# Two of a sample's four loads issued by ScalarE, the small constants sent behind the first weights, and a later place for one block's inverse root

## The chip, the cores and the metric

The kernel runs on one core of a Trainium2 chip. The metric is the device time of one execution in microseconds (us). A core has five engines with a queue of instructions each: TensorE (PE in the profile; its weight loads are PEld), VectorE (DVE), ScalarE (ACT), GpSimd (POOL) and SyncE (SP). SP here only issues DMA transfers; ScalarE and GpSimd can issue them too. An engine runs its queue in order: an instruction that waits holds up all behind it.

## The reference

One encoder layer is applied to a prompt of 1,024 tokens and to a sample of 256 tokens, with one set of weights, all in float32:

```python
h = rmsnorm(x, norm_mix_w)                 # x * rsqrt(mean(x*x) + 1e-6) * w
proj = h @ w_in                            # DeltaNet q/k/v, gates, sg_u, sg_v, branch gates
y_a = deltanet_branch(...) @ w_up_a
y_b = spatial_gating_branch(sg_u, sg_v, ...) @ w_up_b
x = x + (sigmoid(gate_a) * y_a + sigmoid(gate_b) * y_b) @ w_out
x = x + memory_cross_attention(rmsnorm(x), rmsnorm(mem), ...)
x = x + swiglu(rmsnorm(x))                 # then a final rmsnorm
```

Only the very beginning matters here: the first `rmsnorm` of the tokens, the projections to `sg_v` and `sg_u`, and the layer norm and token mixing of the spatial gating branch.

## The kernel before

**Tiling.** Activations lie with features on the 128 partitions: a block of tokens is eight tiles of 128 features by up to 512 tokens. There are three blocks: 0 and 1 are the prompt's halves (512 tokens each), block 2 is the sample (256 tokens). Float32 products are made from three products of a rounded part (`hi`) and a remainder (`lo`) of each operand. `split` (L124) makes them: `hi` on ScalarE, `lo` on VectorE or GpSimd, so every normalised tile takes a VectorE product (L288, tile `nt`), a ScalarE rounding (L125, `hi`) and a subtraction (L126, `lo`).

**The order of the work.** TensorE runs in the order in which the program is written. The other engines' orders are made by a planner, which works from the written order and its own idea of when an operand is ready and may let a ready instruction pass one that it thinks is not. Within the part called `begin` (L399 to L448) ScalarE, GpSimd and VectorE keep the written order among their own instructions there, though the planner can put others between them. The main stream of matmuls is a generator. After each group of matmuls it hands over to `pump` (L71), which runs the side jobs that are due. Due times go by a written clock, `K.clock`, that counts TensorE's time only: a matmul of 264 columns adds 264/2.4 = 110 units, one of 512 columns 213. A side job that yields 2800 goes on after matmuls worth 2,800 units have been written.

**The beginning (L374 to L448).** SP loads the sample `xs` in four transfers of two feature tiles each (L376, 256 KB each), then `sm` (L389, 54.5 KB: norm weights and other small constants), then the first half of the `sg_v` weights in two transfers (`sv_raw0`, L361, 528 KB each), the second half (`second`), block 0 (`x0`, L355) and other constants (`cst`, L394). ScalarE squares the four parts of `xs` (L404), TensorE sums them into means (L413), and ScalarE and VectorE make the inverse root (L416, then three steps L419 to L421). In between, ScalarE splits the first `sg_v` weights (L417, seen as L125 with tile `svh`). Then each of the sample's eight tiles is multiplied by a column of `sm` and the root (L431), rounded (L432) and subtracted (L436), and TensorE starts on real products as they arrive. Before that TensorE is given products of zeros (`hold`, L384). A later line, L479, halves nine columns of `sm` on VectorE. It is written after `begin`, and nothing of the beginning needs its result. Transfers take turns on eight completion semaphores, so each waits for the one that was eight before it.

**The norms of the prompt's blocks.** `other_norms` (L452) is one side job that normalises block 0, block 1 and the memory tokens one after the other. For block 1 and the memory it calls `norm` (L306): eight tiles are squared and added up (`nacc`), and then `rest` (L256) writes small matmuls that sum over partitions (L267), VectorE's root (L270, then ten short steps L225 to L229, result `nst`), a pause `lag2`, matmuls that spread the root over all partitions (L275, shown as `bank<-cst,nst`), and the eight tiles' products and splits, one every 900 units for block 1. `rest` has 2800 as the default of `lag2`; `norm` doesn't set it.

**The main stream beside it.** `sgv(b)` (L571) multiplies a block by the `sg_v` weights, in two halves, one chunk of 128 tokens after the other; each chunk is eight groups of three matmuls and then a GELU (L484 to L487). It is followed by `sgu(0, b)` and `sgu(1, b)` (24 matmuls of 512 columns each). Blocks come in the order 2, 0, 1. `sgv(1)` reads block 1's `hi` and `lo`; `until` (L95) lets side jobs run on until block 1 is marked done. After `sgv(b)` the side job `ln` (L503) normalises that block's chunks: short VectorE steps, a squaring per chunk on ScalarE (L511, `junk`), a root, and a product per chunk on VectorE (L516, `vg`). `mix` (L618) then multiplies `vg` by the token mixing matrix (L625, `bank<-sw,vg`), written 8,000 units after block 0's `ln` is done.

Of the kernel before, what the change touches and what calls it, by code (L numbers as in the profile page):

```python
# [20 lines left out]
NP, NS = 1024, 256  # L21
# [16 lines left out]
S_MIX, S_XA, S_MEM, S_FFN, S_FIN, S_CONV, S_DNW, S_LNW, S_LNB = 0, 8, 16, 24, 32, 40, 100, 101, 105  # L38
# [16 lines left out]
class Trunk:  # L55
# [68 lines left out]
    def split(self, hi, lo, src, eng=None):  # L124
        self.last_hi = self.nc.scalar.activation(hi, src, AF.Copy).ins  # L125
        (eng or self.nc.vector).tensor_tensor(out=lo, in0=src, in1=f32(hi), op=ALU.subtract)  # L126
# [37 lines left out]
def trunk_kernel(ctx: ExitStack, tc: tile.TileContext, a):  # L164
    nc = tc.nc
    V, S, G, T, SY = nc.vector, nc.scalar, nc.gpsimd, nc.tensor, nc.sync
# [3 lines left out]
    def pool(name, bufs=1, **kw):  # L170
        if kw.get("space") != DRAM:
            kw["reuse_waits"] = "tile"
        return tc.tile_pool(name=name, bufs=bufs, **kw)
# [12 lines left out]
    n = 0  # L186
# [31 lines left out]
    def bank(p=pq, tag="b"):  # L218
        return p.tile([P, 512], F32, tag=tag, name="bank")
# [83 lines left out]
        rsqrt(y, ms, sc)  # L303
        yield lag2

    def norm(p, xk, n, wcol, sink, pace=1300, step=700, lag=1500):  # L306
        nm = Norm(p, n)
        for k in range(KT):
            nm.add(xk(k))
            yield step  # L310
        yield from nm.rest(xk, wcol, sink, pace, lag=lag)

    def to_h(h, b):
        return lambda k, t: split(h[b][0][:, k, :], h[b][1][:, k, :], t, V if k % 2 else G)

    def act_tiles(p=None):

        p = p or hp
        return [
            (  # L320
                p.tile([P, KT, n], F32R, tag=f"hi{b}", name=f"hi{b}"),
                p.tile([P, KT, n], F32R, tag=f"lo{b}", name=f"lo{b}"),
            )
            for b, (_, n) in enumerate(BLOCKS)
        ]
# [23 lines left out]
    xp = ses.enter_context(pool("xin"))  # L349
    sv = []  # L350

    def x_load(src, t0, n, name):
        x = xp.tile([P, KT, 512], F32, tag="x", name=name)[:, :, :n]
        for k in range(0, KT, 2):
            SY.dma_start(x[:, k : k + 2, :], src[:, k : k + 2, t0 : t0 + n])  # L355
        return x

    def sv_raw(half, raws=None):
        raws = [K.raw() for _ in range(2)] if raws is None else raws
        for i, raw in enumerate(raws):  # L360
            SY.dma_start(raw, a["w_sv"][half][:, i * 1056 : (i + 1) * 1056])  # L361
        return raws
# [10 lines left out]

    xs = hp.tile([P, KT, NS], F32, tag="lo1", name="xs")  # L374
    for k in range(0, KT, 2):
        SY.dma_start(xs[:, k : k + 2, :], a["xT"][:, k : k + 2, NP:])  # L376
    h05 = cp.tile([P, 13], F32, name="h05")
    fixed = h05[:, 9:12]
    for i, v in enumerate((1.0 / D, EPS, 0.0)):
# [4 lines left out]
    def hold(n, room):  # L384
        for _ in range(n):
            T.matmul(room, zero.to_broadcast([P, P]), zero.to_broadcast([P, room.shape[1]]), start=True, stop=True)

    hold(3, bank())
    SY.dma_start(sm, a["small"])  # L389
    sv_raw0 = sv_raw(0)  # L390
    second = hp.tile([P, 2, 1056], F32, tag="hi1", name="second")
    sv_raw1 = sv_raw(1, [second[:, i, :] for i in range(2)])
    x0 = x_load(a["xT"], 0, 512, "x0")
# [2 lines left out]
    x_h = act_tiles()  # L396
# [28 lines left out]
    for k in range(KT):  # L425
# [8 lines left out]
        while los and (k == KT - 1 or los[0][0] < k):  # L434
            n, t = los.pop(0)
# [16 lines left out]
    def other_norms():  # L452
        nm = Norm(xp, 512)
        nm.acc = squares[:, 0, :]
        yield from nm.rest(lambda k: x0[:, k, :], S_MIX, to_h(x_h, 0), 600, lag=LAG0, halves=2)
        done.add(0)
        x1_ = x_load(a["xT"], 512, 512, "x1")
        yield 3000
        yield from norm(xp, lambda k: x1_[:, k, :], 512, S_MIX, to_h(x_h, 1), 900, lag=4500)
        done.add(1)  # L460
        mem = x_load(a["memT"], 0, 512, "mem")
        yield 6000
        yield from norm(xp, lambda k: mem[:, k, :], 512, S_MEM, lambda k, t: SY.dma_start(md[k], t))

    norms = K.side(other_norms())


# [1990 lines left out]
```

## Time and profile before

| | us |
|---|---|
| median of 3 runs | 2195.53 (2195.31 to 2195.96) |
| the profiled execution | 2195.64 |
| its span, first to last instruction | 2193.9 |
| PE busy in the span | 2176.9 (99%) |
| DVE, ACT, POOL busy | 1357.6, 880.1, 572.9 |
| granted TensorE clock (share of full speed) | 0.999 |

The profiled execution's time is 1.74 us more than its span, what lies around the first and last instruction. "Busy" of PE counts from the start of a matmul to its modelled end, and consecutive matmuls overlap, so the real rate is read from the distance between starts. In a timeline row the columns are start, length, engine, line, operation, written and read tiles with their shape, the number of instructions that were merged, and in brackets the engine's idle time before it with what ended it. Transfers issued by an engine appear as that engine with a "q" (SPq, ACTq); their length is that of issuing, not of moving the data.

### The profile page before, as it was taken

Reading aid. Unit: us, or ns where it says so; the run is one execution under the profiler, and the core shown is the slowest. Engines: PE = TensorE matmul, PEld = TensorE weight load, DVE = VectorE, ACT = ScalarE, POOL = GpSimd, SP = SyncE. Lnnn points to the kernel's source line nnn. Section 1 sums busy time; section 2 is a strip of 40 time slices with the busy share of each in tenths; the row PEclk is TensorE's granted clock in tenths of the full one; section 3 lists DMA queues with packets and bytes.
Section 4 is the critical chain, followed back from the end, with each engine's and each line's share of the span. In section 5 each row is a group of like instructions: output and inputs, shape, how many; then the busy total and the mean of one; then the engine's idle time right before and its main releaser. Section 6 shows DMA issues by size and latency. Waiting matters only on the chain.

```text
span 2193.9 us, 32384 instructions
## 1 busy us (share of the span) xinstructions
PE 2176.9 (99%) x12436; PEld 1905.0 (87%) x12436; DVE 1357.6 (62%) x2614; ACT 880.1 (40%) x1648; POOL 572.9 (26%) x379
## 2 busy tenths in 40 slices
PE   9999999999999999999999999999999999999998
PEld 8888888898888899888988888888888888888888
DVE  7868587686874845677644546644434444378575
ACT  6433262544535453124544433332322222343454
POOL 3010010100000000042412332566666665200031
PEclk9999999999999999999999999999999999999999
DMA  5221412323234546741522421222222222493631
GB/s 194 92 93 57 118 54 94 82 66 93 75 119 124 169 138 209 238 144 43 188 68 107 162 98 63 102 84 87 82 77 77 85 96 91 138 347 125 206 111 58
DMA packets 188309, 255.13 MB, mean 116 GB/s; under 512 B 71978, under 2 KB 102266, under 8 KB 188154
## 3 DMA queue, kind: packets, MB, share of 16 engines
q1 hardware_dynamic: 170618, 228.15, 31.7%
q10 hardware_dynamic: 17536, 24.91, 3.1%
q8 instruction: 97, 1.59, 0.3%
q14 instruction: 58, 0.48, 0.1%
HBM read 179.05 MB, written 73.97 MB: 115 GB/s over the span
## 4 chain that ended last, share of the span: by engine, by line
PE 90%; DVE 4%; ACT 2%; DMA 1%; issue 1%; POOL 0%; DVEq 0%; SPq 0%; ACTq 0%
PE bank L108 89%; PE bank L121 1%; DVE acc L689 1%; DVE U L931 1%; DMA braw<-gq 1%; DVE zt L923 0%; ACT U L913 0%; ACT UT L910 0%; ACT hi L125 0%; DVE lo L126 0%; DVE gb L810 0%; DVE gs L689 0%; ACT acc L687 0%; ACT gs L692 0%; ACT whi L125 0%
## 5 line engine op out<-in xcount | busy, mean ns | idle before, releaser
L108 PE MATMUL bank<-hi,whi 128*128 128x512 f32 (+1 forms) x1976 | 701.7, 355 | 0.2 <-DVE vg L487 0.2
L108 PE MATMUL bank<-hi,wlo 128*128 128x512 f32 (+1 forms) x1976 | 687.1, 348 | 0.0
L108 PE MATMUL bank<-lo,whi 128*128 128x512 f32 (+1 forms) x1976 | 686.9, 348 | 0.0
L108 PEld LDWEIGHTS bank<-hi,wlo 128*128 128x128 f32 x1976 | 373.5, 189 | 48.7
L108 PEld LDWEIGHTS bank<-hi,whi 128*128 128x128 f32 x1976 | 374.4, 189 | 44.8 <-DVE vg L487 1.0
L108 PEld LDWEIGHTS bank<-lo,whi 128*128 128x128 f32 x1976 | 374.6, 190 | 43.1
L125 ACT ACTIVATE whi<-raw 128x1024 fp32r<-128x1024 f32 (+1 forms) x136 | 136.9, 1009 | 252.5 <-PE bank L108 225.1
L126 POOL TENSOR_TENSOR wlo<-raw,whi 128x1024 fp32r<-128x1024 f32 x65 | 159.5, 2455 | 290.4 <-ACT whi L125 290.4
L108 PE MATMUL bank<-bhl,whi 128*128 128x512 f32 x408 | 125.9, 390 | 0.0
L126 DVE TENSOR_TENSOR wlo<-raw,whi 128x1024 fp32r<-128x1024 f32 (+1 forms) x71 | 80.7, 1139 | 69.5 <-ACT whi L125 66.8
L126 POOL TENSOR_TENSOR wlo<-x,whi 128x1024 fp32r<-128x1024 f32 x40 | 97.5, 2436 | 46.7 <-ACT whi L125 46.7
L2091 DVE TENSOR_TENSOR x<-x,bank 128x512 f32<-128x512 f32 x21 | 14.4, 688 | 124.3 <-ACT x L1886 124.3
L689 DVE SCALAR_TENSOR_TENSOR acc<-craw,sm,acc 128x510 f32<-128x510 f32 (+1 forms) x96 | 73.8, 769 | 27.6 <-ACT acc L687 25.9
L108 PEld LDWEIGHTS bank<-bhl,whi 128*128 128x128 f32 x408 | 76.4, 188 | 16.4 <-ACT whi L125 0.4
L1899 DVE SCALAR_TENSOR_TENSOR t<-t,x 128x512 f32<-128x512 f32 x42 | 64.4, 1534 | 28.4 <-ACT t L1898 28.4
L125 ACT ACTIVATE whi<-x 128x1024 fp32r<-128x1024 f32 (+1 forms) x48 | 49.2, 1026 | 78.1 <-PE bank L108 70.1
L108 PE MATMUL bank<-bhl,wlo 128*128 128x512 f32 x204 | 79.6, 390 | 0.5 <-DVE wlo L126 0.5
L1908 DVE SCALAR_TENSOR_TENSOR t<-bank,t 128x512 f32<-128x512 f32 (+1 forms) x44 | 24.5, 558 | 82.6 <-PE bank L108 82.6
L108 PE MATMUL bank<-bhl,ahl 128*128 128x512 f32 x312 | 75.0, 395 | 0.0
L1050 ACT ACTIVATE gs<-bank 128x512 f32<-128x512 f32 (+1 forms) x60 | 31.2, 519 | 102.9 <-PE bank L108 93.5
L108 PEld LDWEIGHTS bank<-bhl,ahl 128*128 128x128 f32 x312 | 58.7, 188 | 13.6
L1886 ACT ACTIVATE x<-bank 128x512 f32<-128x512 f32 x63 | 37.6, 597 | 82.0 <-PE bank L108 79.8
(411 smaller groups left out, 4517.3 us busy)
## 6 DMA issues: line engine op xcount, KB each, us to landing
raw<-in_w_gu SPq DMA_DIRECT2D x44, 512.0 KB, 3.3
braw<-gq SPq DMA_DIRECT2D x14, 1024.0 KB, 7.5
raw<-in_w_g SPq DMA_DIRECT2D x20, 512.0 KB, 3.3
gq<-t SPq DMA_DIRECT2D x33, 256.0 KB, 2.1
gtd<-gs ACTq DMA_DIRECT2D x32, 256.0 KB, 2.3
w<-in_w_dn SPq DMA_DIRECT2D x8, 1024.0 KB, 12.6
raw<-in_w_qkv SPq DMA_DIRECT2D x12, 512.0 KB, 3.4
gq<-r SPq DMA_DIRECT2D x22, 256.0 KB, 2.0
```

The lines of the kernel that those rows point to most:

```text
L108: self.nc.tensor.matmul(out, l, r, start=start, stop=stop, skip_group_check=more)
L121: self.nc.tensor.transpose(out, x, ident)
L125: self.last_hi = self.nc.scalar.activation(hi, src, AF.Copy).ins
L126: (eng or self.nc.vector).tensor_tensor(out=lo, in0=src, in1=f32(hi), op=ALU.subtract)
L689: V.scalar_tensor_tensor(out=dst, in0=src, scalar=wj, in1=dst, op0=ALU.mult, op1=ALU.add)
L931: V.scalar_tensor_tensor(out=U[d][:, hs, :], in0=quad(pu), scalar=mine[:, 2 * level + d : 2 * level + d + 1], in1=U[d][:, hs, :], op0=ALU. ...
L1050: S.activation(t, ps, AF.Tanh, scale=0.5)
L1886: S.activation(t, ps, AF.Copy)
L1899: V.scalar_tensor_tensor(out=t, in0=t, scalar=1.0, in1=src, op0=ALU.add, op1=ALU.mult)
L1908: V.scalar_tensor_tensor(out=out, in0=u, scalar=sign, in1=t, op0=ALU.mult, op1=ALU.mult)
L2091: V.tensor_tensor(out=c22, in0=c22, in1=pe, op=ALU.add)
```

## The change

The second and fourth load of `xs` are issued by ScalarE in place of SP. The load of `sm` moves behind the two loads of `sv_raw0` in SP's order. `norm` takes the pause `lag2` as an argument, 2800 by default, and block 1's call sets it to 5000, so that the spreading matmuls and all that follows them in that side job are written later. Block 0 (which calls `rest` directly) and the memory tokens keep 2800.

```diff
-    def norm(p, xk, n, wcol, sink, pace=1300, step=700, lag=1500):
+    def norm(p, xk, n, wcol, sink, pace=1300, step=700, lag=1500, lag2=2800):
         nm = Norm(p, n)
         for k in range(KT):
             nm.add(xk(k))
             yield step
-        yield from nm.rest(xk, wcol, sink, pace, lag=lag)
+        yield from nm.rest(xk, wcol, sink, pace, lag=lag, lag2=lag2)
...
     for k in range(0, KT, 2):
-        SY.dma_start(xs[:, k : k + 2, :], a["xT"][:, k : k + 2, NP:])
+        (S if k % 4 else SY).dma_start(xs[:, k : k + 2, :], a["xT"][:, k : k + 2, NP:])
...
     hold(3, bank())
+    sv_raw0 = sv_raw(0)
     SY.dma_start(sm, a["small"])
-    sv_raw0 = sv_raw(0)
     second = hp.tile([P, 2, 1056], F32, tag="hi1", name="second")
...
-        yield from norm(xp, lambda k: x1_[:, k, :], 512, S_MIX, to_h(x_h, 1), 900, lag=4500)
+        yield from norm(xp, lambda k: x1_[:, k, :], 512, S_MIX, to_h(x_h, 1), 900, lag=4500, lag2=5000)
```

## The prediction

> **What bounds the kernel now.** The page first, for how much there is to win:
>
> ```profile
> span 2193.9 us, 32384 instructions
> PE 2176.9 (99%) x12436; PEld 1905.0 (87%) x12436; DVE 1357.6 (62%) x2614; ACT 880.1 (40%) x1648; POOL 572.9 (26%) x379
> ```
>
> TensorE sets the time. All its idle time is 2193.9 - 2176.9 = 17.0 us, 0.8% of the span, so a change that only moves work can win no more than that, and this one touches the first 100 us. The waits of PE in the first 130 us come next (total, times, longest):
>
> ```profile
> PE bank L108 <- DVE ab L607: 1.6, 1, 1.6
> ...
> PE bank L108 <- POOL lo L126: 0.7, 1, 0.7
> ...
> PE bank L108 <- DVE vg L516: 0.4, 1, 0.4
> ```
>
> Which wait is whose is read from the timeline. The beginning, up to the first real product:
>
> ```profile
> 0.73 1.28 ACT L382 ACT_TABLE_LOAD   x1 [0.73 <-PEq L2446]
> 0.74 1.97 SPq L376 DMA_DIRECT2D xs<-in_xT  x4
> 2.75 0.47 SPq L389 DMA_DIRECT2D sm<-in_small  x1
> 3.26 0.91 SPq L361 DMA_DIRECT2D raw<-in_w_sv  x2
> 3.52 1.39 ACT L404 ACTIVATE first<-xs 128x512 f32<-128x512 f32 x2 [1.29 <-DMA xs<-in_xT]
> 6.30 1.37 ACT L404 ACTIVATE first<-xs 128x512 f32<-128x512 f32 x2 [1.39 <-DMA xs<-in_xT]
> 7.32 0.17 DVE L479 TENSOR_SCALAR h<-sm 128x9 f32<-128x9 f32 x1 [1.69 <-DMA sm<-in_small]
> 9.07 0.47 ACT L416 ACTIVATE seed<-bank,h 128x256 f32<-128x256 f32 x1 [1.41 <-PE bank L108]
> 9.26 0.76 SPq L394 DMA_DIRECT2D cst<-in_const  x1
> 9.45 2.21 ACT L125 ACTIVATE svh<-raw 128x1056 fp32r<-128x1056 f32 x2
> 9.58 0.43 DVE L419 SCALAR_TENSOR_TENSOR bank<-bank,seed 128x256 f32<-128x256 f32 x1 [2.09 <-ACT seed L416]
> 10.98 0.88 DVE L431 SCALAR_TENSOR_TENSOR bank<-xs,sm,bank 128x256 f32<-128x256 f32 x2
> 11.56 0.72 ACT L432 ACTIVATE hi<-bank 128x256 fp32r<-128x256 f32 x2
> 11.98 0.51 PE L108 MATMUL bank<-svh,hi 128*128 128x264 f32 x2 [0.42 <-ACT hi L432]
> ```
>
> Two chains meet at 11.56. One is the sample's: third quarter of `xs` at 6.30, squares, means, root (9.07), three VectorE steps, first product with `sm` (10.98). The other is ScalarE's splitting of the first weights, 9.45 to 11.66. `sm` itself landed by 7.32, and L479, which nobody here needs, took it while VectorE had nothing to do.
>
> How fast the loads come, as the issue list of the first 30 us (size, median us to landing) and the busy shares of two stretches (last column GB/s) have it, and what issuing costs ScalarE later in the kernel (ns, least/median/most):
>
> ```profile
> raw<-in_w_sv SPq DMA_DIRECT2D x2, 528.0 KB, 6.4
> ```
> ```profile
> 1.75:2.50 0.75, 0.75 (x2) 0.34 (x1) 0.00 (x0) 0.47 (x2) 0.00 (x0) 1.00 0.67 139
> 2.50:3.75 1.25, 1.25 (x3) 0.41 (x2) 0.00 (x0) 0.23 (x1) 0.00 (x0) 1.00 1.00 340
> ```
> ```profile
> L1053 ACTq DMA_DIRECT2D gtd<-gs x48: 326/326/527, 256.9 to 723.8; - x48
> ```
>
> The stream is full from 2.5 us on. Two weight loads issued at 3.26 and half of 0.91 later, 6.4 on the median, land near 9.3 and 10.5; `cst`, which waits for the first of them, goes out at 9.26.
>
> Now block 1's root. PE's rows, then VectorE's:
>
> ```profile
> 55.59 0.95 PE L108 MATMUL bank<-cst,nacc 128*128 128x1 f32 x8
> ...
> 59.62 0.28 PE L108 MATMUL bank<-svl,hi 128*128 128x264 f32 x1
> 61.52 1.13 PE L108 MATMUL bank<-cst,nst 128*128 128x128 f32 x8 [1.62 <-DVE ab L607]
> 62.40 0.37 PE L108 MATMUL bank<-svh,hi 128*128 128x264 f32 x1
> ...
> 65.03 0.40 PE L108 MATMUL bank<-hi,whi 128*128 128x512 f32 x1
> ```
> ```profile
> 59.99 0.41 DVE L485 SCALAR_TENSOR_TENSOR gt<-gt,bank 128x248 f32<-128x248 f32 x1 [1.16 <-ACT gt L484]
> ...
> 61.21 0.16 DVE L229 SCALAR_TENSOR_TENSOR nst<-bank,nst 128x4 f32<-128x4 f32 x1
> ...
> 62.75 2.07 DVE L288 SCALAR_TENSOR_TENSOR nt<-x,sm,bank 128x512 f32<-128x512 f32 x3 [1.30 <-issue]
> ...
> 68.25 0.40 DVE L487 SCALAR_TENSOR_TENSOR vg<-gt,bank 128x248 f32<-128x248 f32 x1
> ...
> 76.72 0.68 DVE L126 TENSOR_TENSOR lo<-nt,hi 128x512 fp32r<-128x512 f32 x1
> ...
> 78.42 1.91 DVE L516 TENSOR_SCALAR vg<-vg,sums 128x512 f32<-128x512 f32 x4
> ```
>
> The row that names L607 as releaser is the root's: its last step L229 ends at 61.37, and the spreading matmuls start at 61.52. The root is late because VectorE's queue holds a GELU step of a chunk (59.99) ahead of its last steps, and that chunk's matmuls end only just before the spread. PE stands for 1.62 us. A second, smaller place is 17 us later:
>
> ```profile
> 79.02 1.86 PE L108 MATMUL bank<-sw,vg 128*128 128x128 f32 x8 [0.41 <-DVE vg L516]
> 80.63 0.36 PE L108 MATMUL bank<-svh,hi 128*128 128x264 f32 x1
> ...
> 85.06 1.05 PE L108 MATMUL bank<-sw,vg 128*128 128x128 f32 x8
> 85.88 0.37 PE L108 MATMUL bank<-svh,hi 128*128 128x264 f32 x1
> ```
>
> Token mixing waits for block 0's `vg`: 0.41 us shown as idle, and the same eight matmuls then hold PE for 80.63 - 79.02 = 1.61 us where the next set takes 85.88 - 85.06 = 0.82, so 0.8 more are spent waiting chunk by chunk. Together 1.2 us.
>
> **The root, sent later.** No instruction is added or removed, the order of TensorE's queue changes. Between the sums (55.59) and the spread lie nine groups of three matmuls: the first count of groups whose 330 units each pass 2800. For 5000 it is sixteen (15 x 330 = 4950 is short of it). The seven groups from 62.40 to 65.03 are the rest of `sgv(0)`, so the spread lands exactly behind them, ahead of `sgu(0, 0)`. They fill PE from 59.74 (59.62 and one spacing of 0.12) to about 59.74 + 2.6 = 62.3. The root, if VectorE's order is as it was, is done at 61.37: no wait, and 0.9 us of room. **-1.6 us**. VectorE, ScalarE and GpSimd get the spread at 62.3 + 0.88 = 63.2 in place of 62.4, which is 0.8 later in time, and 2.4 later against PE's own progress.
>
> What is queued behind it: block 1's eight `nt`, `hi`, `lo`, then the memory's load and norm, all in one side job, and beside them block 0's `ln`. By the written clock `ln`'s first steps lay behind five of the eight `nt` and its root behind seven; with the later spread they lie behind three and five. More weighty is the last chunk's GELU. Its ScalarE and squaring rows were
>
> ```profile
> 65.39 0.36 ACT L484 ACTIVATE gt<-bank 128x248 f32<-128x248 f32 x1
> ...
> 70.70 0.71 ACT L511 ACTIVATE junk<-vg,sums 128x512 f32<-128x512 f32 x1
> ```
>
> that is, behind three `hi`, and its last step L487 came at 68.25. The chunk's matmuls now end near 62.4, before the first `nt` exists, and ScalarE and VectorE are free there, so I expect L487 near 64 and `ln`'s squares from about 66, four to five us sooner. Then `vg`, 78.42 - 70.70 = 7.7 us behind the squares, starts near 74, and PE, 1.6 us earlier, wants it at 77.4: the 1.2 us of the second place go too. Bounds: nothing of it goes (and more comes, third rival), or all. I take all, since the margin is 3 us: **-1.2 us**. Block 1's last `lo` was done at 77.4, 15.0 us behind the end of the spread; 63.2 + 15.0 = 78.2, and PE will want it at 80.63 - 2.8 = 77.8. That would be 0.4 late, but the last two `hi` stood behind the four squares, which move forward, so I cost it at nothing. The memory's norm goes about 3 us later; its products are stored and read long after; its own root has the same pause of 2800 and could run into a GELU step as block 1's did, at most 1.6 us again. I take nothing, since its last step and spread now fit without idle.
>
> **The loads of `xs`.** Moving two issues to ScalarE costs it 0.33 to 0.53 us each before its table load (0.73, 1.28 us long; its first squares start at 3.52), hidden by the wait for `xs`: ready at 0.73 + 1.0 + 1.28 = 3.0. It is worth what an earlier start gives. SP took 0.49 for each of four, so the last is issued 1.0 us sooner at most. But the stream is full from 2.5 on, so only the slow start can be filled: 0.75 us x (340 - 139) GB/s = 150 KB, or 0.45 us. So `xs` and what is behind it come 0 to 0.45 us sooner; I take 0.3. The Trainium skill ("DMA: Bandwidth & Descriptors", section "Issuing engines are not separate DMA queues") says that transfers issued by different engines run on the same 16 DMA engines, and that issuing from several saves only the time of issuing. By it this part would be worth at most those 1.0 us, by the rows 0.45; the full stream of this trace agrees with it, and it speaks against any gain in the rate.
>
> The sample's chain then gains 0.3, and the ScalarE chain too, since the first weights (landing 9.3 and 10.5, used at 9.45 and about 10.5) are in the same stream. Alone this part is **-0.3**, bounds -0.45 and 0.
>
> **`sm` behind 1.08 MB of weights.** It landed by 7.32 right behind `xs`; now it follows the second weight load, 10.5 - 0.3 = 10.2. Bounds: 8.6, if that load's earlier issue counted in full (0.74 + 3 x 0.49 = 2.2, and 6.4), and 10.9, without the gain and trailing by 0.4 as it did behind `xs`, whose last quarter was squared from 6.9. Two instructions read it. L431 needs it at 10.98: no loss. L479 stands in VectorE's queue ahead of L419. If it stays, L419 goes from 9.58 to 10.2 + 0.2 = 10.4, and the three steps, L431, `hi` and PE's first product go with it: **+0.8**, bounds -0.3 (8.6, with the gain above in its place) and +1.5. If the planner sets it elsewhere, the -0.3 stays. The planner put it there because it held `sm` to be ready early; `sm` is still fifth in SP's queue, so I take it to stay. This replaces the -0.3, as the later chain decides.
>
> **The sum.** -1.6 - 1.2 + 0.8 = -2.0 us on the profiled execution's 2195.64 (span 2193.9 and 1.74 around it), that is 2193.6. It lay 0.11 above the median of the runs, so I predict **2193.5**.
>
> **The rivals.** First, the sample starts sooner: L479 is elsewhere, or `sm` lands by 9.3. For it speaks that its place is the planner's and not written; against it that VectorE is idle before L419. -2.8 - 0.3 = -3.1, so 2192.4.
>
> Second, slower: the wait moves to token mixing. Place: `vg` of block 0. If the planner leaves `ln` behind the same `nt` as before, `vg` comes 0.8 later with the spread, the mixing starts at 79.8 in place of 79.02, and PE waits there for all that it won: +0.8 from this part, +0.8 from `sm`, 2195.53 + 1.6 = 2197.1. It decides once `vg` starts later than 77.4. For it speaks that the whole stretch from 62.75 to 79.02 is one VectorE and ScalarE chain; against it the early GELU.
>
> Third, the planner's orders change far beyond 130 us, because its own times shift. With 17.0 us of idle in all and orders of all engines in play, 5 us either way are possible; nothing in the profile speaks for a side, but a longer queue has more ways to be worse.
>
> **How the numbers follow.** Forecast 0.45, first rival 0.25, second 0.17, third 0.13. The range goes from 2191.8 (first rival with the full 0.45 and half a us of spread) to 2197.2, the second; under 0.2 is left out, mostly of the third. The forecast alone has 2192.4 (no loss by `sm`) to 2194.2 (`sm` at +1.5). A measurement tells about 0.2%, or 4.4 us, from no change. All cases but the third lie within it; of the third I give 0.04 to faster, 0.07 to slower, 0.02 within: 0.04, 0.89, 0.07.
>
> **What would show it.** Right: no PE idle ahead of `bank<-cst,nst` near 62, `junk` from about 66, `bank<-sw,vg` near 76.5 with no idle and 0.82 long; two ACTq rows near 0.7; L479 at about 10.2 and PE's first real product near 12.8. Wrong: L479 behind L421 or later, and the first product by 11.7 (first rival); idle at `bank<-sw,vg` of 2 us or more (second); waits of PE behind 130 us that are not in the waits now (third); or a wait of PE for a `lo` of block 1 near 78.

## The result, and the profile after

The changed kernel takes 2204.49 us (median of 5 runs, 2202.20 to 2205.16) against 2195.53 (5 runs, 2195.31 to 2196.62). The medians lie 9.0 us apart; the ratio is estimated at 1.0036, or 7.9 us, with a 95% interval of 1.0025 to 1.0047, or 5.5 to 10.3 us. The change makes the kernel slower. The forecast was 2193.5 and the range ended at 2197.2.

From the page of the changed kernel (its profiled execution took 2205.16), the span and the first row of busy times:

```profile
span 2203.3 us, 32382 instructions
PE 2181.2 (99%) x12436; PEld 1909.8 (87%) x12436; DVE 1356.1 (62%) x2614; ACT 879.2 (40%) x1648; POOL 572.7 (26%) x379
```

The span grew by 9.4 us. TensorE's idle time grew by 5.1 us, from 17.0 to 2203.3 - 2181.2 = 22.1. The other 4.3 stand as busy time (2181.2 - 2176.9), though TensorE runs the same 12436 matmuls: it ran some of them more slowly. The waits of PE in the changed kernel say where it idles (total, times, longest):

```profile
PE bank L108 <- DVE gm L555: 2.7, 1, 2.7
PE bank L108 <- DVE vg L516: 2.7, 1, 2.7
PE bank L108 <- DVE vg L487: 1.3, 1, 1.3
```

The wait for the root (L607, 1.6 us) is gone. In its place stand 2.7 us for block 0's `vg` at the token mixing, and 2.7 us at a place that the prediction never looked at: `gm` (L555), the gates' decays that `decays` (L521) computes beside `sgu` and block 1's `ln`. The rows of PE at these places:

```profile
63.35 1.05 PE L108 MATMUL bank<-cst,nst 128*128 128x128 f32 x8
64.16 0.47 PE L108 MATMUL bank<-hi,whi 128*128 128x512 f32 x1
...
81.09 2.16 PE L108 MATMUL bank<-sw,vg 128*128 128x128 f32 x8 [2.69 <-DVE vg L516]
82.91 0.57 PE L108 MATMUL bank<-svh,hi 128*128 128x264 f32 x1
83.27 0.42 PE L108 MATMUL bank<-svh,lo 128*128 128x264 f32 x1
83.49 0.42 PE L108 MATMUL bank<-svl,hi 128*128 128x264 f32 x1
...
124.12 0.83 PE L108 MATMUL bank<-cst,gm 128*40 128x128 f32 x4 [2.74 <-DVE gm L555]
```

The last of these places in the kernel before:

```profile
116.86 0.63 PE L108 MATMUL bank<-cst,gm 128*40 128x128 f32 x4
```

Read as a list of leads and lags: `sgu(0, 0)` starts 0.87 us sooner than before (65.03, now 64.16). The first group behind the mixing starts 2.28 later (80.63, now 82.91) and the `gm` products 7.26 later (116.86, now 124.12), though only 2.74 of that is their own stall. So something between the stalls costs time too. Why is seen in the windows of PE (length, busy time, granted clock, DMA share, GB/s):

```profile
80.00:82.00 2.00, 0.91 (x4) 0.51 0.63 141
82.00:84.00 2.00, 2.00 (x11) 0.50 1.04 414
84.00:86.00 2.00, 2.00 (x11) 0.50 1.01 395
86.00:88.00 2.00, 2.00 (x15) 0.78 0.60 234
...
124.00:126.00 2.00, 1.88 (x9) 0.60 0.71 260
126.00:128.00 2.00, 2.00 (x9) 0.54 0.07 20
```

Behind each of these two stalls the granted clock falls to half for some us, and matmuls start 0.22 us apart (83.27, 83.49) in place of the 0.12 of before. An estimate of the loss is busy time by the missing share of the clock: 0.91 x 0.49 + 2 x 0.50 + 2 x 0.50 + 2 x 0.22 = 2.9 us behind the first stall and 1.88 x 0.40 + 2 x 0.46 = 1.7 behind the second. (The same sum behind the wait of 1.3 us near 28 gives 1.3. The three together, 5.9, are more than the 4.3 by which busy time grew, so the estimate is on the high side.) With that 1.7 the lag of 7.26 becomes 9.0 of the 9.4 us. Behind 130 us the listed waits of PE differ in one line alone: 1.2 us for `wlo` (L126) where the kernel before has 0.5.

**Why `vg` is late.** ScalarE's first square of `ln` in the changed kernel and the VectorE step that it waited for:

```profile
67.84 1.25 DVE L507 TENSOR_SCALAR sums<-sums 128x4 f32<-128x4 f32 x1
69.19 0.72 ACT L511 ACTIVATE junk<-vg,sums 128x512 f32<-128x512 f32 x1 [1.53 <-DVE sums L507]
```

VectorE's rows of the changed kernel from the layer norm's variance (L512) to `vg`, then GpSimd's in the same stretch and further on:

```profile
72.16 0.17 DVE L512 TENSOR_SCALAR sums<-sums 128x4 f32<-128x4 f32 x1 [1.02 <-ACT junk L511]
...
73.44 1.26 DVE L229 SCALAR_TENSOR_TENSOR sums<-sums 128x4 f32<-128x4 f32 x1
...
76.63 1.23 DVE L229 SCALAR_TENSOR_TENSOR sums<-sums 128x4 f32<-128x4 f32 x1
...
80.50 1.91 DVE L516 TENSOR_SCALAR vg<-vg,sums 128x512 f32<-128x512 f32 x4
```
```profile
73.24 1.44 POOL L126 TENSOR_TENSOR lo<-nt,hi 128x512 fp32r<-128x512 f32 x1 [4.18 <-ACT hi L125]
76.10 1.74 POOL L126 TENSOR_TENSOR lo<-nt,hi 128x512 fp32r<-128x512 f32 x1 [1.42 <-ACT hi L125]
115.32 2.46 POOL L126 TENSOR_TENSOR wlo<-raw,whi 128x1024 fp32r<-128x1024 f32 x1 [37.47 <-ACT whi L125]
120.64 2.36 POOL L126 TENSOR_TENSOR wlo<-raw,whi 128x1024 fp32r<-128x1024 f32 x1 [2.86 <-ACT whi L125]
```

The same chain in the kernel before (it ends with `vg` at 78.42):

```profile
73.65 0.17 DVE L512 TENSOR_SCALAR sums<-sums 128x4 f32<-128x4 f32 x1 [0.94 <-ACT junk L511]
...
74.26 1.27 DVE L228 TENSOR_TENSOR sums<-sums 128x4 f32<-128x4 f32 x1
```

L512 comes 1.5 us sooner than before, as `ln` does start earlier. But the ten short steps of its root share VectorE with products (`nt`), subtractions (`lo`) and GELU steps of `sgu`. Between L512 and `vg` there were three of these, of about 0.7 us each, in the kernel before; now there are eight. And two short steps last 1.2 us in place of 0.16, each until GpSimd's subtraction beside it ends (73.24 + 1.44 = 74.68, 76.10 + 1.74 = 77.84); the kernel before had one such step (74.26). From L512 to `vg` it takes 80.50 - 72.16 = 8.3 us; before it was 78.42 - 73.65 = 4.8. So the larger part of the added 3.5 us is the five further steps, and about 1.1 the second long one. L507 is a long step too, ahead of the squares.

**Why `gm` is late.** This chain, too, is made of short VectorE steps. VectorE's rows of the changed kernel from the first step of the decays to the last, then those of the kernel before:

```profile
110.73 0.24 DVE L537 TENSOR_TENSOR wk<-ab,rows 128x80 f32<-128x80 f32 x1
...
112.01 0.73 DVE L288 SCALAR_TENSOR_TENSOR nt<-mem,sm,bank 128x512 f32<-128x512 f32 x1
...
115.44 2.36 DVE L229 SCALAR_TENSOR_TENSOR sums<-sums 128x4 f32<-128x4 f32 x1
...
120.63 2.65 DVE L516 TENSOR_SCALAR vg<-vg,sums 128x512 f32<-128x512 f32 x1
...
123.81 0.43 DVE L555 SCALAR_TENSOR_TENSOR gm<-wk,rows 128x32 f32<-128x32 f32 x4
```
```profile
106.28 0.24 DVE L537 TENSOR_TENSOR wk<-ab,rows 128x80 f32<-128x80 f32 x1
...
110.97 2.35 DVE L228 TENSOR_TENSOR sums<-sums 128x4 f32<-128x4 f32 x1
...
114.61 0.44 DVE L555 SCALAR_TENSOR_TENSOR gm<-wk,rows 128x32 f32<-128x32 f32 x4
```

The chain took 8.3 us before and 13.1 now. Products of the memory's norm stand in it (112.01), and, longer, it has run into GpSimd's second subtraction of weights (120.64), where a product of block 1's `ln` just ahead of the chain's last steps stands for 2.65 us. Before, the chain met only the first of the two (GpSimd's at 110.88); the second began at 116.44, behind `gm`.

### The profile page after: what moved, and what is told of

Same layout as the page of the kernel before. It is cut to its first block, busy times and chain, and to the rows that moved or that the text cites. A ratio compares the mean times of both kernels' runs of the same rounds, so it can differ in the third digit from the quotient of the medians.

```text
span 2203.3 us, 32382 instructions
## 1 busy us (share of the span) xinstructions
PE 2181.2 (99%) x12436; PEld 1909.8 (87%) x12436; DVE 1356.1 (62%) x2614; ACT 879.2 (40%) x1648; POOL 572.7 (26%) x379
## 4 chain that ended last, share of the span: by engine, by line
PE 91%; DVE 5%; ACT 2%; DMA 1%; issue 1%; DVEq 0%; SPq 0%; ACTq 0%
PE bank L108 90%; PE bank L121 1%; DVE acc L689 1%; DMA braw<-gq 1%; DVE U L931 1%; DVE zt L923 0%; DVE nt L288 0%; ACT U L913 0%; ACT UT L910 0%; ACT junk L511 0%; DVE lo L126 0%; DVE sums L229 0%; ACT hi L125 0%; DVE gb L810 0%; DVE gs L689 0%
## 5 line engine op out<-in xcount | busy, mean ns | idle before, releaser
L126 POOL TENSOR_TENSOR wlo<-raw,whi 128x1024 fp32r<-128x1024 f32 x65 | 159.3, 2453 | 297.1 <-ACT whi L125 297.1
L126 DVE TENSOR_TENSOR wlo<-raw,whi 128x1024 fp32r<-128x1024 f32 (+1 forms) x71 | 80.6, 1138 | 69.9 <-ACT whi L125 69.7
L126 POOL TENSOR_TENSOR wlo<-x,whi 128x1024 fp32r<-128x1024 f32 x40 | 97.6, 2440 | 46.8 <-ACT whi L125 46.8
```

## The experiments

Medians of the kernel before, run again with each set of experiments, went from 2195.61 to 2196.32 us, so differences between sets are good to some 0.7 us.

**The parts alone.** The theory from the traces was that the later root costs the time (A); the rival, that the loads do it by reshuffling the planner's orders (B). Loads alone:

```diff
-    yield from norm(xp, ..., lag=4500, lag2=5000)
+    yield from norm(xp, ..., lag=4500)
```

> Both edits of the loads, and the root's pause back at 2800. Theory A (the later root costs the time: it moves block 0's ln, the memory's norm and so the waits for vg at the token mixing and for gm of the decays): both waits of 2.7 us are gone, the wait for ab (L607) of 1.6 us is back, the spacing of the matmuls behind 82 us is 0.12, and the time is 1 to 2.5 us above before (the 1.26 us wait for vg of the GELU near 28, a little of clock, +0.2 at the first product), so 2196.5 to 2198. Theory B (the loads reshuffle the planner's order and that costs it): the waits near 80 and 117 us are there in this kernel too, and the time is 6 to 9 us above before, 2201.5 to 2204.5.

Measured: 2194.84 us against 2195.85, ratio 0.9998 (0.9988 to 1.0007). Neither late wait is there. The wait near 28 us is there, and yet it costs nothing, as two rows of PE in that kernel show:

```profile
29.80 0.39 PE L108 MATMUL bank<-hi,whi 128*128 128x256 f32 x1 [1.26 <-DVE vg L487]
...
61.52 0.68 PE L108 MATMUL bank<-cst,nst 128*128 128x128 f32 x4 [1.12 <-DVE nst L229]
```

The spread starts at 61.52, just as before: the wait of 0.7 for a `lo` is not there, and the root's wait shrank from 1.62 to 1.12 and swallowed the rest of what the beginning had lost. Theory A's 1 to 2.5 us above before were too many. Next the late root alone (the pause of 5000 with the loads as before; "the late root" from here on):

```diff
-    yield from norm(xp, ..., lag=4500)
+    yield from norm(xp, ..., lag=4500, lag2=5000)
```

> The pause of 5000 for block 1 alone, the loads as before. Theory A: the waits of 2.7 us at the token mixing (vg, L516) and at the gm matmul (L555) are there, the granted clock falls behind them, and the time is 6 to 9 us above before, 2201.5 to 2204.5; the wait of 1.3 us at the GELU near 28 is not there. Theory B: no such waits, and the time is 0 to 2 us below before, 2193.5 to 2195.5. If both parts are needed for the collision, e1 and e2 each stay within 2 us of before.

Measured: 2203.01 us, ratio 1.0034 (1.0022 to 1.0045), 7.2 above before. Both waits are there, 2.7 us each, and the one near 28 is not. A holds, B falls: one number in one call makes the loss. The changed kernel, run again later (e17 below), lies just as far above its own runs of before, 7.2 us. The two edits of the loads one by one, first the issue by ScalarE:

```diff
-    SY.dma_start(xs[...], a["xT"][...])
+    (S if k % 4 else SY).dma_start(xs[...], a["xT"][...])
```

> Only the two loads of xs issued by ScalarE; sm ahead of the weights and the pause of 2800 as before. Theory A with the order of the bias products as the cause near 28 us: the order of L612 and L616 among the GELU steps is changed here as in the changed kernel, so the wait of 1.26 us for vg (L487) near 28 is here, the mean matmuls start 0.6 us later than before, and the time is 1 to 2.5 us above before. Rival: the wait near 28 comes of sm's place, then it is not here, and the time is within 0.5 us of before.

Measured: 2197.17 us, ratio 1.0005 (0.9995 to 1.0014), 1.3 above before, which the runs can't tell from none. The wait near 28 us is there (1.3 for L487), so it comes with the issue and not with `sm`. Then `sm` alone:

```diff
+    sv_raw0 = sv_raw(0)
     SY.dma_start(sm, a["small"])
-    sv_raw0 = sv_raw(0)
```

> Only sm behind the first two weight loads, all four loads of xs by SP. VectorE's order differs in one place: L419 stands ahead of L479. So sm costs nothing: it is read by L479 and L431 only, the first real product comes at 11.9 to 12.1 as before, and the time is within 0.4 us of before. By the prediction's term of +0.8 (L479 holds the root's steps until sm lands) the first product comes at 12.8 and the time is 0.8 us above before.

Measured: 2196.35 us, ratio 1.0001 (0.9992 to 1.0011); the first product came at 11.94. The +0.8 that I had laid on `sm` is not there, but this run doesn't try its reason: the planner set L479 behind L419 here (9.97 and 9.49), so `sm` could hold up nothing.

**The two collisions, each taken away.** From here on the base is the late root alone (2203.0). The memory's norm, put back to its old place in TensorE's order:

```diff
-        yield 6000
+        yield 4000
         yield from norm(xp, lambda k: mem[:, k, :], ...)
```

> The late root alone (pause 5000), and the pause ahead of the memory's norm cut from 6000 to 4000, so that the memory's sums and spread stand in TensorE's order behind as many matmuls as in the kernel before. Theory A1 (the shifted memory norm collides with the decays' chain on VectorE and makes gm late): the wait for gm (L555) of 2.7 us and the low clock from 120 to 129 us are gone, worth 2.7 + 3.1 = 5.8 us, the wait for vg (L516) near 80 stays; 2203 - 5.8 = 2197.2. Rival: the decays are late because all of PE's progress there is (the mixing's wait), then the gm wait stays at 2 us or more and the time is 2202 to 2204.

Measured: 2198.56 us, ratio 1.0010 (1.0001 to 1.0020), 4.5 less, of the 5.8 expected. The wait for `gm` is gone, that for `vg` is there unchanged (2.69). The opposite test, on the kernel before with its early root:

```diff
-        yield 6000
+        yield 8500
```

> The kernel before with its early root, and only the pause ahead of the memory's norm raised from 6000 to 8500, so that the memory's sums and spread stand in TensorE's order where the late root puts them. Theory A1: the wait for gm (L555) appears with 2 to 3 us and the clock falls behind it, no wait at the mixing beyond the 0.4 us of before; 2195.85 + 5.8 = 2201.6. Rival (the gm wait needs the late mixing too): no wait for gm over 0.5 us, 2195 to 2196.5.

Measured: 2199.77 us, ratio 1.0016 (1.0007 to 1.0026), 3.7 above before. Its waits of PE now name both the old wait for the root and the one for `gm`:

```profile
PE bank L108 <- DVE gm L555: 2.7, 1, 2.7
PE bank L108 <- DVE ab L607: 1.6, 1, 1.6
```

So the place of the memory's norm alone decides over `gm`; the root and the mixing have no part in it. It cost 3.7 and not 5.8. In the profiled execution, the fastest of the ten, the clock stayed at 1.00 behind this stall. The other collision, with the first mixing of block 0 written later:

```diff
-        yield MIX + (0, 1500, 1000)[b]
+        yield MIX + (0, 1500, 1000)[b] + (2500 if g == 0 and b == 0 else 0)
```

> The late root alone, and the first token mixing of block 0 written 2,500 units later (seven groups of matmuls more ahead of it). Theory A2 (vg of block 0 comes 2.7 us too late, and nothing behind it suffers from a later mixing): the wait for vg near 80 falls to 0.4 us or less, the clock stays at 1.00 there, worth 2.7 + 1.7 = 4.4 us; the wait for gm stays; 2203 - 4.4 = 2198.6. Rival: the wait only moves, to the lo of block 1 or to the next mixing, and the time is 2201.5 to 2203.5.

Measured: 2201.35 us, ratio 1.0022 (1.0013 to 1.0032), 1.7 less in place of 4.4, and close to the rival's forecast. The wait for `vg` is gone, but two thirds of it went to what stands behind it, as PE's rows show:

```profile
79.50 0.39 PE L108 MATMUL bank<-svh,hi 128*128 128x264 f32 x1 [1.50 <-ACT hi L125]
80.22 0.39 PE L108 MATMUL bank<-svh,lo 128*128 128x264 f32 x1 [0.34 <-DVE lo L126]
```

Block 1's last `hi` and `lo` are late too, hidden until now behind the wait for `vg`. Both cures together on the late root (pause 3300 for the memory, which gives the old place here):

```diff
-        yield 6000
+        yield 3300
...
-        yield MIX + (0, 1500, 1000)[b]
+        yield MIX + (0, 1500, 1000)[b] + (2500 if g == 0 and b == 0 else 0)
```

> The late root (pause 5000) with both cures: the first mixing of block 0 written 2,500 units later, and the memory's norm back at its old place in TensorE's order (pause 3300). Theory A1 and A2 together: neither the wait for vg nor that for gm, the wait of 1.5 + 0.3 us for block 1's hi and lo stays; 2203.0 - 4.45 - 1.66 = 2196.9, so the late root cured is 0.5 to 1.5 us above before. Rival (the two waits share a cause, and a cure of both wins less than the sum): 2198.5 or more.

Measured: 2196.34 us, ratio 1.0002 (0.9993 to 1.0011); the two cures add up, within the spread of the runs (4.5 + 1.7 alone, 6.7 together). The same two edits on the changed kernel with its loads (e16), and the changed kernel itself beside it (e17):

> The changed kernel with its loads, its late root, and both cures (first mixing 2,500 units later, memory's pause 3300). If the two collisions are the whole of the loss: neither the wait for vg (L516) nor that for gm, the wait of 1.3 us near 28 and that of 1.5 us for block 1's hi stay, and the time is 1 to 3 us above before, 2196.5 to 2198.5. Rival (with the loads in place something else costs it): 2200 or more.

> The changed kernel as it is, for a comparison on the same chip with its cured form: 2202 to 2206, waits of 2.7 us for vg and for gm.

Measured: 2195.64 us, ratio 1.0000 (0.9992 to 1.0009), against 2203.54, ratio 1.0036 (1.0023 to 1.0050); that is a little below the 2196.5 to 2198.5 expected. The waits for `vg` at the mixing and for `gm` are gone, those near 28 and for block 1's `hi` stay, as expected. The two collisions, with the clock behind them, are the whole loss as far as the runs can tell.

**The clock.** Products of zeros fill TensorE's two stalls on the late root:

```diff
-        pr = bank()
+        pr = bank(); hold(3, pr)
...
-        pmx = bank()
+        pmx = bank(); hold(3 if (g, b) == (0, 0) else 0, pmx)
```

> The late root alone, with three products of zeros of 512 columns (about 0.83 us each) ahead of the first mixing of block 0 and three ahead of the gm products, into the banks that these then overwrite. They add work only where TensorE waits. Theory C (the idle of 2.7 us is what lowers the granted clock): the idle at both places falls to about 0.2 to 0.5 us, the clock stays at 1.00 behind both, and the lost clock of 1.7 and 3.1 us is won: 2203 - 4.8 = 2198.2. Rival (the clock falls for another cause, such as the transfers of these windows or the sort of work): windows at 0.50 stay, and the time is 2202 to 2204.

Measured: 2199.67 us, ratio 1.0015 (1.0005 to 1.0024), 3.3 less than without them (4.8 were expected, from the windows of one execution), though `vg` is as late as it was (the mixing starts at 80.20, on the late root at 80.01). PE's rows, the products of zeros being L386, and the windows behind them:

```profile
77.34 2.75 PE L386 MATMUL bank<-h 128*128 128x512 f32 x6
80.20 1.85 PE L108 MATMUL bank<-sw,vg 128*128 128x128 f32 x8
...
118.32 2.75 PE L386 MATMUL bank<-h 128*128 128x512 f32 x6
121.22 0.63 PE L108 MATMUL bank<-cst,gm 128*40 128x128 f32 x4 [0.16 <-DVE gm L555]
```
```profile
82.00:84.00 2.00, 2.00 (x19) 1.00 1.01 395
...
122.00:124.00 2.00, 2.00 (x16) 1.00 0.34 135
```

The granted clock is 1.00, in these and every other window from 78 to 88 and from 116 to 130 us. Nor is that one execution's luck: the mean granted clock of all ten runs is 0.998 or 0.999, that of the late root's six 0.996 to 0.998. The transfers still run (DMA share 1.01 from 82 to 84), so they alone do not lower it. It is TensorE's idling that lowers the clock, and the loss of the late root closes: two waits of 2.7 less the waits removed, 5.4 - 1.62 - 0.41 = 3.4 us, and 3.3 of clock, 6.7 of the 7.2.

**How late is too late.** The pause at 3900, twelve groups, which leaves the memory's norm in its old place:

```diff
-    yield from norm(xp, ..., lag=4500, lag2=5000)
+    yield from norm(xp, ..., lag=4500, lag2=3900)
```

> The pause at 3900 (twelve groups in place of nine or sixteen), loads as before; the memory's sums and spread then stay where they were in TensorE's order. Theory D (the chain on VectorE and ScalarE from the spread at 61.5 to vg at 79 is what bounds this stretch, so TensorE's gain at the root is lost at the mixing): the wait ahead of the spread falls from 1.62 to about 0.5, the wait for vg (L516) rises from 0.4 to about 1.5, no wait for gm, and the time is within 1 us of before. Rival (the middle place wins what the late one lost by going too far): both waits fall, 1.5 to 2.5 us below before.

Measured: 2195.76 us, ratio 1.0001 (0.9992 to 1.0009). The rows of PE:

```profile
62.00 1.13 PE L108 MATMUL bank<-cst,nst 128*128 128x128 f32 x8 [0.54 <-DVE ab L607]
...
78.96 1.86 PE L108 MATMUL bank<-sw,vg 128*128 128x128 f32 x8 [0.95 <-DVE vg L516]
```

The root's wait fell from 1.62 to 0.54, and the mixing's rose from 0.41 to 0.95 (1.5 were expected): `vg` comes at 78.4 in both kernels, and so the mixing starts at 79.0 in both. Theory D holds. Two tries at a version below both kernels follow. Thirteen groups, the mixing 1,500 units later, the memory in its old place (4700):

```diff
-    yield from norm(xp, ..., lag=4500, lag2=5000)
+    yield from norm(xp, ..., lag=4500, lag2=4200)
...
-        yield 6000
+        yield 4700
...
-        yield MIX + (0, 1500, 1000)[b]
+        yield MIX + (0, 1500, 1000)[b] + (1500 if g == 0 and b == 0 else 0)
```

> A try at a version below both: pause 4200 (thirteen groups), the first mixing of block 0 written 1,500 units later, the memory's norm at its old place in TensorE's order (pause 4700). If the chain of theory D has some room for block 1's hi and lo: the wait ahead of the spread 0.2 to 0.5, none for vg, 0.3 to 1 for hi or lo, no wait for gm, and 1 to 2 us below before, 2194 to 2195. If the chain has none: the wait moves to block 1's hi and lo with 1 to 2 us, and the time is within 0.7 us of before.

Measured: 2196.12 us (2193.23 to 2198.57), ratio 0.9999 (0.9990 to 1.0008). The wait for `vg` was 1.0 even so, since `vg` itself came at 79.3; neither of the two forecasts had that. And with a shorter chain: first a test on the late root whether GpSimd's subtractions are what makes VectorE's short steps long.

```diff
-    split(..., V if k % 2 else G)
+    split(..., V if k % 2 or b == 1 else G)
```

> The late root alone, and all eight subtractions (lo) of block 1 on VectorE; four of them were GpSimd's. Theory E (VectorE's short steps of 0.16 us that last 1.24 to 1.25 us at 66.8, 72.4 and 75.6 do so since GpSimd's subtraction holds what they share): these steps last 0.15 to 0.17 us here, 3 x 1.1 = 3.3 us are won and 4 x 0.6 = 2.4 us of subtractions added, so vg starts about 0.9 us sooner, the wait at the mixing is 1.5 to 2.0, and the time is 0.5 to 1.5 us below the late root's 2203. Rival (the steps are long for another cause): some step of L229 or L507 there still lasts over 1 us, vg starts 2.4 us later, and the time is 2 to 3 us above the late root's.

Measured: 2201.28 us, ratio 1.0023 (1.0012 to 1.0033), 1.7 less than the late root. GpSimd has no work there now, and the VectorE step that was long at 75.6 on the late root is:

```profile
75.70 0.16 DVE L229 SCALAR_TENSOR_TENSOR sums<-sums 128x4 f32<-128x4 f32 x1
```

No such step is long any more, L507 with 0.17 among them; `vg` starts 0.9 us sooner (79.42, here 78.49), as theory E has it, and the wait is 1.6 in place of 2.7. So GpSimd's subtractions do make these steps long, but without them `vg` is still late: the same subtractions now take VectorE's time. With the same edit, the pause at 3900:

> A second try at a version below both: pause 3900, loads as before, and all subtractions of block 1 on VectorE. Theory D with E: the chain to vg is 0.9 us shorter without GpSimd's subtractions, so vg comes near 77.5 to 78, the wait ahead of the spread is 0.5, that for vg 0 to 0.4, no wait for gm, and the time is 1 to 2 us below before, 2194 to 2195. Rival (VectorE's added work makes the chain as long as it was): the wait for vg is 0.9 or more, and the time is within 0.5 us of before.

Measured: 2197.37 us, ratio 1.0005 (0.9996 to 1.0014), with 1.7 us of wait for `vg`, which started at 78.6. The rival held in the wait, though not to the 0.5 us in time: with the spread 1.5 us sooner than in e14 (61.5 against 63.0), `vg` came no sooner. No version measurably below the kernel before was found.

## Why the prediction was wrong

**What failed is the step of -1.2**, as the prediction put it: "`vg`, 78.42 - 70.70 = 7.7 us behind the squares, starts near 74", with a margin of 3 us. L487 did come early (64.10 on the late root, 65.18 in the changed kernel; "near 64" was right). But the squares started at 69.19, not 66 (68.11 on the late root), held up by L507, which lay behind `nt` and `lo` and lasted 1.25 us. And `vg` stood 80.50 - 69.19 = 11.3 us behind them, not 7.7. I had carried over the length of a chain of short dependent steps from one trace, as if it were the chain's own. It is set by what stands between the steps: three products, subtractions and GELU steps from L512 on before, eight after, and two steps held by GpSimd in place of one. So `vg` came 6.5 us behind the expected 74 (1.1 of it the changed kernel had lost before, its sums for the root starting at 56.66 and not 55.59; on the late root `vg` came at 79.42). The term of -1.2 was +2.3 (a wait of 2.69 in place of 0.41) and more by the clock.

**"I take nothing" for the memory's norm** was the second failure, and the larger one: a term put at nothing. I asked only what its own root could wait for, not whose VectorE time its products would take. Put back, it wins 4.5 us (e5); moved alone, it costs 3.7 (e11).

**The clock** was in no term. The prediction costed a stall at its length; on the late root the two cost 3.3 us more (e7).

**What was right:** no wait ahead of the spread, and the -1.6 there; on the late root alone the spread starts at 62.28, as worked out (62.3). Block 1's last `lo`, "0.4 late" and costed at nothing, was later than that (1.50 and 0.34 in e6), hidden behind `vg`.

**The loads.** The -0.3 was not there, and the +0.8 for `sm` neither. These are rows of the changed kernel's beginning:

```profile
4.45 1.15 ACT L404 ACTIVATE first<-xs 128x512 f32<-128x512 f32 x2 [1.17 <-DMA xs<-in_xT]
5.85 1.15 ACT L404 ACTIVATE first<-xs 128x512 f32<-128x512 f32 x2 [0.25 <-DMA xs<-in_xT]
9.10 0.17 DVE L479 TENSOR_SCALAR h<-sm 128x9 f32<-128x9 f32 x1 [2.78 <-DMA sm<-in_small]
...
9.84 0.43 DVE L419 SCALAR_TENSOR_TENSOR bank<-bank,seed 128x256 f32<-128x256 f32 x1 [0.57 <-ACT seed L416]
12.20 0.50 PE L108 MATMUL bank<-svh,hi 128*128 128x264 f32 x2 [0.39 <-ACT hi L432]
```

The third quarter of `xs` is squared 0.45 us sooner than before (6.30, now 5.85), the bound worked out from the full stream, but the first 0.93 later (3.52, now 4.45; 4.84 and 4.47 in e1 and e3): loads that share the stream land closer together. That agrees with the rule that the prediction took from the Trainium skill ("DMA: Bandwidth & Descriptors", section "Issuing engines are not separate DMA queues"). The first product comes 0.2 later. L479 did stay ahead of L419, as assumed, but `sm` had landed by 9.10, within the bounds (8.6 to 10.9) and ahead of the root's first step, so L479 held up nothing. The wait of 1.26 near 28, from another order of the planner's, was not foreseen. All of this is lost in the root's stall behind it: e1 can't be told from before.

**The rivals.** The first had its condition (`sm` by 9.3) and not its gain: the first product came at 12.20, not by 11.7. The second named the place and the point (`vg` later than 77.4) and priced it at 0.8 us; the third gave orders changing beyond 130 us no mechanism, and the trace shows 0.7 us of new waits there. The true course was the second, with a second stall of the same kind and the clock on top, and none of the three reached past 2200.5.

## What to carry to other kernels

A wait that is removed at the head of a chain on another engine can come back at the chain's end: ask when the chain's last product comes, not only when its first input does (e8: 1.1 us less wait at the root, `vg` at 78.4 as before, no gain). Where one side job does several things one after the other, a pause in the first moves all the others, and each meets other work; hold the later ones in their place (e5, e12). A stall of TensorE of 1 to 3 us can cost its own length once more, or more than that, by the clock. By the estimate above it was 3.1 us behind 2.74 in e2's execution and 3.0 behind 1.26 in e16's. A few products of zeros in the stall win that part back (e7).

## What the runs showed of the hardware

**The clock's fall isn't certain.** Idle times of 1.26 to 2.7 us were followed by some us at a granted clock of 0.50 in some executions and by none in others: 1.26 us near 28 lowered it in the changed kernel and not in e17, the same kernel, nor in e1; and 2.7 us at `gm` lowered it in e2 and not in e11. The runs of one kernel spread accordingly: of the eleven of e16, the six up to 2195.64 us had a mean granted clock of 0.999, the five from 2196.96 to 2198.87 one of 0.998 or 0.997. The Trainium skill ("TensorE: Matmul & The Clock Gate", section "What's actually happening") says that the clock goes to half after at least one idle window of about 3.4 us, and that the windows run freely. The half is what the rows show; the length is not: 2.7 us and less were enough here. That the phase of the windows makes the difference between executions is a guess that no run here tests.

**VectorE's short steps behind GpSimd.** In these traces a step of 0.16 us lasted 1.2 to 2.4 us, to the end of the GpSimd subtraction that had started just before it (73.44 + 1.26 = 74.70 and 73.24 + 1.44 = 74.68), and where GpSimd had nothing to do (e14, up to `vg`) none did. The Trainium skill ("SBUF — State Buffer", section "SBUF: two separate sides") calls the port pair that the two share an exclusive lock, held for the whole instruction, which these rows agree with.
